# The input projection of a hybrid layer in seven-product form, in three token groups, with the recurrence one group behind

## The chip, the cores and the metric

The kernel runs on one core of a Trainium2 chip. Its time is the device time of one execution in microseconds (us), the median of several runs. The engines are named as in the profile: PE is TensorE's matmul, PEld its weight load, DVE VectorE, ACT ScalarE, POOL GpSimd, SP SyncE, which here only issues DMAs.

## The reference

One layer of a streaming encoder, over 2048 prompt frames (16 tiles of 128 tokens) and 8 streams of 16 frames (one more tile, the "sample" tile, number 16). D_MODEL is 1024.

```
h   = RMSNorm(x);  P = h @ w_in   -> q|k|v (3*512) | z (512) | b, a (4+4) | B, C, H (3*512)
group A: causal conv of 4 taps + SiLU on q, k, v; L2 norm of q and k; beta = sigmoid(b), decay g from a
  per chunk: A = strict lower part of (beta k) k^T * decay;  solve (I + A) [u, w] = [beta v, beta k e^g]
    v_new = u - w S;   o = (q e^g) S + (q k^T * decay) v_new;   S = S e^(g_last) + k_tail^T v_new
  o = RMSNorm_head(o) * SiLU(z)
group B: y = B * causal_conv3(C * H)
x = x + RMSNorm(concat(o, y) @ w_o)
x = x + RMSNorm(SwiGLU(RMSNorm(x)))
```

Outputs are y for prompt and sample tokens, the convolutions' last rows, and the recurrent states (4 heads of 128 x 128) of the prompt and of each stream.

## The kernel before

Every large product is made to f32 accuracy from pieces that run at the fast rate: each operand is split into a high part and a remainder ("hi", "lo"), and a product becomes three matmuls, hi x hi, hi x lo and lo x hi.

**Projection** (0 to 958 us). The 17 tiles are taken in six groups, `GROUPS`: three of three prompt tiles, one of two, and the first, which holds tiles 0, 1 and the sample tile; a group is 384 tokens wide, the one of two 256. For each group the 28 blocks of 128 output channels are made one by one by `project`: 8 parts of the inner dimension times 3 matmuls, 24 in one PSUM bank (`dbank`, three of them), by the helper `mm3` (L141). `weights` casts a block (ACT, L344) and subtracts (L346, half on GpSimd and half on VectorE), and stores the pair in DRAM (`wsplit`), from which most later groups load it. `x_first` and `x_prep` bring a group's x in (L211: the cast of the high part). After each block, `conv_qkv` copies it from PSUM, applies the four taps (`taps`, L372, on VectorE) and a SiLU; the results of a group stay in SBUF.

**Recurrence.** Within each group: `pair_stage` makes k k^T and k q^T of each tile and inverts 32 x 32 blocks on VectorE; `level_stage` (L586, L596, L601) joins the blocks; `chunk_stage` carries the state S from tile to tile: products L641, L648, L655 on the chain from S to the next S with `r` (L643, L644), `yt` (L650) and the update (L658), and L662 and L667 beside it for the output. `sample_stage` does the same for the eight streams. The order is written out by hand: the last chunk of a group is held over and done at the start of the next, so that products of the projection are always at hand between the steps of a chain.

**Output tiles** (958 to 1190). `o_tile` multiplies a tile by `w_o` (L818), adds the residual, and makes the FFN's input; the first eight run alone, the others beside the FFN's preparation. **FFN** (from about 1190): gate-up (L1034, weight sums and splits L1000 to L1010, x parts L938 to L942, combinations L1076 to L1106) in three groups of 6, 6 and 5 tiles, then down (L1192). Both already use the seven-product form.

That form cuts both matrices in two by two blocks (inner dimension in halves, outputs or tokens in halves). Seven products of sums of blocks, instead of eight of blocks, give the four result blocks after some additions. It costs sums of weight blocks, sums of token blocks and combinations of results.

A scheduler orders the instructions of each engine when the program is built. PSUM has eight banks: `psd` 3, `pst` 2, `psg` 2, `pso` 1.

Of the kernel before, what the change touches and what calls it, by code (L numbers as in the profile page):

```python
# [33 lines left out]
WF = W1 + NS * 3  # L34
TLS = True
O_SPLIT = 8
NPD, NPT, NPG = 3, 2, 2
NR, NKV = 3, 2
XKB = 4
# [33 lines left out]
def kernel(  # L73
# [4 lines left out]
    xs0,  # L78
# [29 lines left out]
    mixd = [dram.tile([P, KD, P], F32, name=f"mixd{t}") for t in range(NT)]  # L108
    wsplit = [dram.tile([P, 2, KD, P], F32, name=f"wsplit{j}") for j in range(28)]
# [36 lines left out]
    with ExitStack() as ph:  # L146
# [3 lines left out]
        wk = ph.enter_context(tc.tile_pool(name="wk", bufs=1))  # L150
        small = ph.enter_context(tc.tile_pool(name="small", bufs=2))

        def obank():
            return pso.tile([P, 512], F32, tag="o", name="obank")
# [6 lines left out]

        S = gp.tile([P, H, P], F32, tag="S", name="S_init", bufs=2)
        V.memset(S, 0.0)
        junkq = gp.tile([P, P], BF16, name="junkq")
        junko = gp.tile([P, P], BF16, name="junko")

        inner = ph.enter_context(ExitStack())
        psg = inner.enter_context(tc.tile_pool(name="psg", bufs=NPG, space=PSUM))
        pso = inner.enter_context(tc.tile_pool(name="pso", bufs=8 - NPD - NPT - NPG, space=PSUM))
        dp = inner.enter_context(tc.tile_pool(name="dp", bufs=1))  # L170
        hp = inner.enter_context(tc.tile_pool(name="hp", bufs=KD + 3))
        wp = inner.enter_context(tc.tile_pool(name="wp", bufs=2))
        cp = inner.enter_context(tc.tile_pool(name="cp", bufs=2))

        def spread(r, n):
            c = n * P
            rg = cp.tile([P, W1], F32, tag="xk", name="rg", bufs=XKB)
            V.tensor_mul(rg[:, :c].rearrange("p (t i) -> p t i", t=n), ident.unsqueeze(1).broadcast_to([P, n, P]),
                         r.unsqueeze(2).broadcast_to([P, n, P]))
            ps = tbank()  # L180
            T.matmul(ps[:, :c], ones, rg[:, :c], start=True, stop=True)
            rb = small.tile([P, W1], F32, tag="rb", name="rb")
            A.copy(rb[:, :c], ps[:, :c])
            return rb

        def x_prep(tiles):
            n = len(tiles)
            c = n * P
            ss = small.tile([P, MAXT], F32, tag="xss", name="xss")
            s2 = small.tile([P, MAXT], F32, tag="xs2", name="xs2")  # L190
            for i, t in enumerate(tiles):
                for q in range(2):
                    xt = cp.tile([P, D // 2], F32, tag="x", name="xt")
                    with tc.issue_after(wloads[-20 + 2 * i + q].ins):
                        nc.sync.dma_start(out=xt, in_=x[t, :, q * 512:(q + 1) * 512])
                    if q:
                        V.scalar_tensor_tensor(xt, xt, 1.0, xt, op0=ALU.mult, op1=ALU.mult, accum_out=s2[:, i:i + 1])
                    else:
                        A.activation(xt, xt, AF.Square, accum_out=ss[:, i:i + 1])
            V.tensor_add(ss[:, :n], ss[:, :n], s2[:, :n])  # L200
            r = rstd(small, ss[:, :n], n, 1.0 / D, EPS, "x")
            rb = spread(r, n)
            hi, lo = [], []
            for k in range(KD):
                xk = cp.tile([P, W1], F32, tag="xk", name="xk", bufs=XKB)
                with tc.issue_after(wloads[-11 + k].ins):
                    nc.sync.dma_start(out=xk[:, :c], in_=xT[k, :, tiles[0] * P:tiles[0] * P + c])
                V.tensor_mul(xk[:, :c], xk[:, :c], rb[:, :c])
                h = hp.tile([P, W1], F32R, tag="hi", name="hi")
                l = hp.tile([P, W1], F32R, tag="lo", name="lo")  # L210
                A.activation(h[:, :c], xk[:, :c], AF.Copy, scale=g_pre[:, k:k + 1])  # L211
                V.scalar_tensor_tensor(l[:, :c], xk[:, :c], g_pre[:, k:k + 1],
                                       h[:, :c].bitcast(F32), op0=ALU.mult, op1=ALU.subtract)
                hi.append(h)
                lo.append(l)
            return hi, lo

        def x_first(tiles):
            n = len(tiles)
            c = n * P  # L220
            hi, lo, sqs = [], [], []
            ps = tbank()
            for k in range(KD):
                raw = ubuf[k] if k < len(ubuf) else gp.tile([P, H, P], F32, tag="dt", name="dt", bufs=2 * MAXT)
                raw = raw.rearrange("p h c -> p (h c)")[:, :c]
                nc.sync.dma_start(out=raw, in_=xs0[k])
                l = hp.tile([P, W1], F32R, tag="lo", name="lo")
                h = hp.tile([P, W1], F32R, tag="hi", name="hi")
                A.activation(h[:, :c], raw, AF.Copy, scale=g_pre[:, k:k + 1])
                V.scalar_tensor_tensor(l[:, :c], raw, g_pre[:, k:k + 1],  # L230
                                       h[:, :c].bitcast(F32), op0=ALU.mult, op1=ALU.subtract)
                hi.append(h)
                lo.append(l)
                xk = cp.tile([P, W1], F32, tag="xk", name="xk", bufs=XKB)
                if k % 2:
                    V.tensor_mul(xk[:, :c], raw, raw)
                    V.tensor_add(xk[:, :c], xk[:, :c], sqs[k - 1][:, :c])
                    for i in range(n):
                        T.matmul(ps[:, 2 * i:2 * i + 1], xk[:, i * P:(i + 1) * P], ones[:, 0:1], start=(k == 1 and i == 0),
                                 stop=(k == KD - 1 and i == n - 1), skip_group_check=True)  # L240
                else:
                    A.activation(xk[:, :c], raw, AF.Square)
                sqs.append(xk)
                if k in (0, 3):
                    fetch()
            r = rstd(small, ps[:, :2 * n].rearrange("p (t c) -> p t c", c=2)[:, :, 0], n, 1.0 / D, EPS, "x")
            return hi, lo, spread(r, n)

        def gate_prep(tiles, hi, lo, rb):
            n = len(tiles)  # L250
            npr = sum(t != SAMPLE for t in tiles)
            c = n * P
            ps = bank() if rb is not None else tbank()
            mm3(ps[:16, :c], [(wba[:, k, :], v[k][:, :c]) for k in range(KD) for v in (hi, lo)])
            bsb = cp.tile([P, W1], F32, tag="xk", name="bsb", bufs=XKB)[:16]
            src = ps[:16, :c]
# [297 lines left out]
        def level_stage(tiles, gt):  # L554
            gt["U"] = []
            for i, t in enumerate(tiles):
# [10 lines left out]
                if s:  # L567
                    continue
# [783 lines left out]
```

## Time and profile before

| | |
|---|---|
| runs | 2606.32, 2605.13, 2602.91 us; median 2605.13 |
| span of the profiled execution | 2604.1 us |
| its own time beside the span | not recorded apart: the three runs above are what there is |
| mean granted TensorE clock | 0.984 |
| DMA | 589.41 MB, mean 226 GB/s |
| projection and recurrence | 0 to 958 us |
| first eight output tiles | 958 to 1190 us |
| FFN, with the other output tiles | 1190 to 2604 us |

A row of a group reads: line, engine, operation, output<-inputs, partitions x elements and types, count, then busy time in us, mean ns of one, and the idle time of the engine in front of them with what ended it. For some f32 matmuls two records stand for one product.

### The profile page before, as it was taken

The page shows a single profiled execution, that of the slowest core. Times are in us where ns is not written, and L with a number is a line of the kernel's source. Part 1 is how long each engine was busy: PE and PEld are TensorE (multiplying, and loading weights), DVE is VectorE, ACT ScalarE, POOL GpSimd, SP SyncE. Part 2 cuts the span into 40 slices and gives each one's busy share as a digit, 9 for nine tenths or more (in the row PEclk, how much of TensorE's full clock was granted, in tenths as well). Part 3 has the DMA queues.
Part 4 walks back from the last instruction along what each step waited for, and adds up shares of the span by engine and source line. Part 5 has one row for each costly group of instructions (what it writes and reads, how often), then busy time and mean ns, then how long its engine had stood idle before and what let it go on. Part 6 is the DMA issues. An engine that isn't in the chain of part 4 may idle for free.

```text
span 2604.1 us, 41820 instructions
## 1 busy us (share of the span) xinstructions
PE 2507.8 (96%) x15061; PEld 2337.2 (90%) x15061; DVE 1741.0 (67%) x3502; ACT 1060.3 (41%) x2570; POOL 632.7 (24%) x580
## 2 busy tenths in 40 slices
PE   8989999999999999999999999999999999999998
PEld 7978899999888988788999999999999988787786
DVE  6876666666586655777888864544655554677588
ACT  6546145162656423444434442222433335333343
POOL 3221101010120101214556610000000035455563
PEclk9999999999999989999999999999999999999999
DMA  7966575847666564678877788877988853333465
GB/s 243 308 246 224 200 280 211 271 162 261 200 225 227 192 218 145 219 235 288 301 251 265 264 273 270 273 247 240 301 270 295 271 180 103 119 121 122 129 216 185
DMA packets 320815, 589.41 MB, mean 226 GB/s; under 512 B 55532, under 2 KB 204720, under 8 KB 301792
## 3 DMA queue, kind: packets, MB, share of 16 engines
q1 hardware_dynamic: 182512, 509.28, 57.8%
q10 hardware_dynamic: 138096, 77.46, 9.9%
q8 instruction: 119, 1.95, 0.3%
q14 instruction: 88, 0.72, 0.1%
HBM read 424.60 MB, written 162.05 MB: 225 GB/s over the span
## 4 chain that ended last, share of the span: by engine, by line
PE 67%; DVE 12%; DMA 10%; ACT 5%; issue 3%; POOL 2%; ACTq 1%; SPq 0%; DVEq 0%; POOLq 0%
PE fbank L1034 30%; PE dbank L141 15%; PE fbank L1192 11%; PE tbank L818 2%; PE dbank L818 2%; DMA xt<-in_x 1%; DMA xk<-in_xT 1%; DVE acc L372 1%; POOL dw L891 1%; ACT L407 1%; DVE Ts L548 1%; DVE pr L546 1%; DMA hTd<-ht 1%; DMA partd<-pt 1%; DMA out_y<-xr 1%
## 5 line engine op out<-in xcount | busy, mean ns | idle before, releaser
L1034 PE MATMUL fbank<-xh,fw 128*128 128x384 f32 (+1 forms) x3696 | 902.1, 327 | 9.2 <-ACT m L1068 5.1
L141 PE MATMUL dbank<-hi,w 128*128 128x384 f32 (+1 forms) x2688 | 689.3, 335 | 15.1 <-ACT w L344 6.2
L1034 PEld LDWEIGHTS fbank<-xh,fw 128*128 128x128 f32 x3696 | 653.7, 189 | 11.3 <-ACT m L1068 5.9
L1034 PE MATMUL fbank<-xl,fw 128*128 128x384 f32 (+1 forms) x1848 | 603.7, 327 | 0.0
L141 PEld LDWEIGHTS dbank<-hi,w 128*128 128x128 f32 x2688 | 482.1, 192 | 22.9 <-ACT w L344 6.6
L1192 PE MATMUL fbank<-dw,as 128*128 128x512 f32 x1980 | 460.7, 394 | 7.7 <-ACT dw L889 2.5
L1192 PEld LDWEIGHTS fbank<-dw,as 128*128 128x128 f32 x1980 | 371.6, 188 | 96.5 <-DVE as L1176 3.7
L141 PE MATMUL dbank<-lo,w 128*128 128x384 f32 (+1 forms) x1344 | 446.7, 332 | 0.1
L1034 PEld LDWEIGHTS fbank<-xl,fw 128*128 128x128 f32 x1848 | 348.7, 189 | 0.0
L141 PEld LDWEIGHTS dbank<-lo,w 128*128 128x128 f32 x1344 | 257.1, 191 | 3.3 <-issue 1.2
L1176 POOL TENSOR_TENSOR as<-ar,as 128x256 fp32r<-128x256 f32 (+1 forms) x207 | 186.7, 912 | 281.9 <-ACT as L1173 281.1
L1151 DVE TENSOR_TENSOR acc<-acc,fbank 128x512 f32<-128x512 f32 x248 | 166.3, 682 | 93.6 <-PE fbank L1192 77.9
L891 POOL TENSOR_TENSOR dw<-dr,dw 128x512 fp32r<-128x512 f32 x52 | 77.0, 1493 | 483.7 <-ACT dw L889 483.5
L1173 ACT CAST as<-ar 128x256 fp32r<-128x256 f32 (+1 forms) x288 | 118.1, 427 | 186.2 <-PE fbank L1192 133.8
L1009 ACT CAST fw<-rg 128x512 fp32r<-128x512 f32 x124 | 77.4, 624 | 190.5 <-PE fbank L1034 156.5
L372 DVE SCALAR_TENSOR_TENSOR acc<-R,cw,acc 128x384 f32<-128x384 f32 (+2 forms) x216 | 132.4, 617 | 11.4 <-ACT acc L403 7.7
L346 POOL TENSOR_TENSOR w<-wr,w 128x512 fp32r<-128x512 f32 x49 | 71.7, 1464 | 240.1 <-ACT w L344 189.8
L1081 DVE TENSOR_TENSOR c<-u,fbank 128x384 f32<-128x384 f32 (+1 forms) x66 | 34.9, 528 | 102.1 <-PE fbank L1034 102.1
L1077 DVE TENSOR_TENSOR m<-m,m 128x384 f32<-128x384 f32 (+1 forms) x44 | 23.1, 526 | 98.2 <-ACT m L1070 98.1
L344 ACT CAST w<-wr 128x512 fp32r<-128x512 f32 x98 | 56.5, 615 | 69.9 <-PE dbank L141 27.1
L546 DVE TENSOR_TENSOR pr<-As,Ts 48x31 f32<-48x31 f32 (+25 forms) x186 | 66.3, 356 | 26.4 <-DMA As<-sa 22.1
L1079 ACT ACTIVATE m<-fbank 128x384 f32<-128x384 f32 (+1 forms) x66 | 31.3, 474 | 121.4 <-PE fbank L1034 114.5
(360 smaller groups left out, 3697.2 us busy)
## 6 DMA issues: line engine op xcount, KB each, us to landing
w<-wsplit SPq DMA_DIRECT2D x119, 1024.0 KB, 5.7
fw<-fsplit SPq DMA_DIRECT2D x188, 512.0 KB, 4.6
fsplit<-fw SPq DMA_DIRECT2D x94, 512.0 KB, 4.9
partd<-pt ACTq DMA_DIRECT2D x88, 384.0 KB, 5.9
rg<-in_w_gu SPq DMA_DIRECT2D x62, 512.0 KB, 3.9
wsplit<-w SPq DMA_DIRECT2D x28, 1024.0 KB, 5.5
wr<-in_w_in SPq DMA_DIRECT2D x98, 256.0 KB, 3.4
ar<-partd SPq DMA_DIRECT2D x48, 384.0 KB, 3.5
```

Source lines behind the costliest of these rows:

```text
L141: T.matmul(ps, l, r, start=(i == 0), stop=(i == n - 1))
L346: e.tensor_tensor(out=wl[:, c], in0=wr, in1=wh[:, c].bitcast(F32), op=ALU.subtract)
L372: V.scalar_tensor_tensor(acc, raw(d), w[:, d:d + 1], acc, op0=ALU.mult, op1=ALU.add)
L546: V.tensor_mul(p3, As[:m, j, j + 1:32].unsqueeze(2).broadcast_to([m, a, b]), Ts[:m, j, 0:b].unsqueeze(1).broadcast_to([m, a, b]))
L818: T.matmul(pss[n], m_[:, j, :], w_[k][:, n * 512:(n + 1) * 512], start=(k == 0 and ci == 0), stop=(k == KD - 1 and ci == 2))
L891: e.tensor_tensor(out=w[:, 1], in0=v, in1=w[:, 0].bitcast(F32), op=ALU.subtract)
L1009: A.copy(w[:, 0], v)
L1034: T.matmul(ps, w_[:, c], b_[k][:, :hw], start=(first and k == 0 and ci == 0), stop=(k == KH - 1 and ci == 2), skip_group_check=not first)
L1151: V.tensor_add(dst, dst, ps)
L1173: ins = A.copy(a[:, 0, :n], v)
L1176: e.tensor_tensor(out=a[:, 1, :n], in0=v, in1=a[:, 0, :n].bitcast(F32), op=ALU.subtract)
L1192: T.matmul(ps, a[:, x_, q * P:(q + 1) * P], w[:, y_], start=(start and q == 0 and ci == 0), stop=(q == c - 1 and ci == 2), skip_group_chec ...
```

## The change

The projection takes the FFN's form and its groups. `GROUPS` becomes 0-5, 6-11 and 12-16 (the sample tile is in the last). The 28 blocks become 14 units of two blocks: k0 k1 v0 v1 q0 q1 z0 z1 C0 H0 B0 C1 H1 B1, each with 7 products of 4 inner parts and 3 matmuls, 84 in four `dbank`s (`psd` 4, `pst` 2, `psg` 2). A matmul is 384 wide, or 320 in the last group. Four sums of weight blocks are made for each unit in the first group; four of the seven split pairs are stored and loaded again in the later groups, and three are split anew. The seven parts of x of the next group are made during units 8 to 13, stored in DRAM (`xpd`) and loaded at the group's start. In the first group the products are made on unnormalized x, and each row is scaled afterwards (L487).

k, q, transposed k and v, SiLU(z) and the short convolution's result go to DRAM on SP's queue and are loaded again. The recurrence becomes a generator, `recur`, over the same arithmetic: a pair step per tile, one inversion for a whole group, then a level step and a chunk step per tile. `steps(n)` issues n of its pieces after each unit of the next group; the last group's follow the first eight output tiles, three after each, and the rest after the eighth. The program's `pack` step drops one copy of x and orders `w_in` by units.

```diff
-GROUPS = [[0, 1, 16], [2, 3, 4], [5, 6, 7], [8, 9, 10], [11, 12], [13, 14, 15]]
+GROUPS = [list(range(0, 6)), list(range(6, 12)), list(range(12, 17))]
...
+UNITS = [(kind, half) for kind in "kvqz" for half in range(2)] + [(kind, half) for half in range(2) for kind in "CHB"]
+STEPS = [[0] * 14, [2, 2, 2, 1, 2, 2, 1, 2, 2, 1, 2, 2, 1, 2], [2, 2, 2, 1, 2, 2, 1, 2, 2, 1, 2, 2, 1, 2]]
-NPD, NPT, NPG = 3, 2, 2
+NPD, NPT, NPG = 4, 2, 2
+NR, NACC, NXK, NWR = 4, 2, 8, 7
...
+        def x_load(gi):
+            hw = len(GROUPS[gi]) * P // 2
+            X = {nm: ([], []) for nm in PARTS}
+            for i, nm in enumerate(PARTS):
+                for k in range(KH):
+                    v = xbuf()[:, :hw]
+                    nc.sync.dma_start(out=v, in_=xpd[gi][i, k])
+                    xsplit(X, nm, k, v, hw, G if k % 4 == 3 else V)
+            return X
...
+        def unit_weights(gi, u):
...
+            if gi == 0:
...
+                V.tensor_sub(s[2], a11, a21)
+                V.tensor_add(s[0], a21, a22)
+                V.tensor_sub(s[1], s[0], a11)
+                V.tensor_sub(s[3], a12, s[1])
...
+            for i, (v, e) in enumerate(((a11, G), (s[2], V), (s[0], G), (s[1], V), (a12, G), (a22, G), (s[3], V))):
+                w = wp.tile([P, 2, 512], F32R, tag="w", name="w", bufs=NWR)
+                if v is None:
+                    nc.sync.dma_start(out=w.bitcast(F32), in_=wsplit[u][:, WSL[i]])
+                else:
+                    A.copy(w[:, 0], v)
+                    (V if first else e).tensor_tensor(out=w[:, 1], in0=v, in1=w[:, 0].bitcast(F32), op=ALU.subtract)
+                    if i in WSL:
+                        nc.sync.dma_start(out=wsplit[u][:, WSL[i]], in_=w.bitcast(F32))
+                yield w[:, 0], w[:, 1]
...
+        def unit(gi, u, X, rb, seg):
...
+            b1, b3, b4, b2 = (psd.tile([P, 512], F32, tag="d", name="dbank")[:, :hw] for _ in range(4))
+            for b, w, nm in zip((b1, b3, b4, b2), W, PARTS):
+                product(b, w, X[nm], True)
...
+            A.copy(s1, b1)
+            A.copy(s7, b3)
+            A.copy(s5, b4)
+            product(b1, W[4], X["B21"], False)
+            product(b3, W[5], X["T4"], False)
+            product(b4, W[6], X["B22"], False)
             fetch()
...
+            V.tensor_add(u2, s1, b2)
+            G.tensor_tensor(out=s7, in0=s7, in1=s5, op=ALU.add)
+            for o, f in places(gi, R[0], 0, seg):
+                A.copy(o, f(b1))
+            for o, f in places(gi, R[1], 0, seg):
+                V.tensor_add(o, f(u2), f(b3))
+            for o, f in places(gi, R[1], 1, seg):
+                G.tensor_tensor(out=o, in0=f(s7), in1=f(u2), op=ALU.add)
+            for o, f in places(gi, R[0], 1, seg):
+                V.tensor_add(o, f(u2), f(b4))
+            if rb is not None:
+                for r in R:
+                    G.tensor_tensor(out=r[:, 3:3 + c], in0=r[:, 3:3 + c], in1=rb[:, :c], op=ALU.mult)
+            return R
...
+        def by_tile(dst, src, n):
+            nc.sync.dma_start(out=dst.rearrange("t p c -> p t c"), in_=src[:, :n * P].rearrange("p (t c) -> p t c", c=P))
...
+        def recur(gi, gt):
+            tiles = GROUPS[gi]
+            for i in range(len(tiles)):
+                pair_step(gi, i, gt)
+                yield
+            yield from solve_steps(gi, gt)
+            for i, t in enumerate(tiles):
+                U = level_step(gi, i, gt)
+                yield
+                if t == SAMPLE:
+                    yield from sample_step(gi, i, gt, U)
+                else:
+                    chunk_step(gi, i, gt, U)
+                yield
...
+            for u, (kind, part) in enumerate(UNITS):
+                R = unit(gi, u, X, rb, kind not in "zB")
+                finish_unit(gi, kind, part, R, gt)
+                if (kind, part) == ("k", 1):
+                    gt.update(gate_prep(gi, X, rb))
+                    key_norms(n, gt)
+                if 7 <= u < 13:
+                    next(prep, None)
+                steps(STEPS[gi][u])
...
+            work.append(recur(gi, gt))
...
         for t in range(O_SPLIT):
             o_tile(t)
+            steps(3)
+        steps(99)
+        nc.scalar.dma_start(out=state_p, in_=state_now[0])
```

`product` is a unit's four inner parts by three matmuls (L440). `finish_unit` calls `convolve` (scale on ACT, taps on VectorE over up to 768 tokens, L507) and stores; for H and B it multiplies on GpSimd (L571, L579). `chunk_step`, `level_step`, `pair_step` and `sample_step` are the former stages for one tile, with loads of what was staged at their head; `solve_steps` is the inversion for the 96 blocks of a group.

More of the change, by code (lines that the diff above doesn't have):

```diff
@@ L171 @@
[L171 to L184, printed above, removed]
@@ L203, in x_prep @@
[L203 to L215, printed above, removed]
@@ L216, in x_prep @@
-            return hi, lo
-        def x_first(tiles):
-            n = len(tiles)
[L220 to L247, printed above, removed]
@@ L262, in gate_prep @@
+            ps = tbank()
             for i in range(n):
@@ new lines, with fetch, product @@
+        worder = [(gi, u) for gi in range(len(GROUPS)) for u in range(len(UNITS))]
+        wpend = []
+        def fetch(n=7):
+            if n == 7 and not worder:
+                return
+            if not wpend or len(wpend[-1][2]) == 7:
+                gi, u = worder.pop(0)
+                wpend.append((gi, u, [], unit_weights(gi, u)))
+            for _ in range(n):
+                wpend[-1][2].append(next(wpend[-1][3]))
+        def product(ps, w, b, first):
+            wh, wl = w
+            bh, bl = b
+            hw = ps.shape[-1]
+            for k in range(KH):
+                c = slice(k * P, (k + 1) * P)
+                for ci, (w_, b_) in enumerate(((wh, bh), (wh, bl), (wl, bh))):
+                    T.matmul(ps, w_[:, c], b_[k][:, :hw], start=(first and k == 0 and ci == 0),
+                             stop=(k == KH - 1 and ci == 2), skip_group_check=not first)
```

825 lines of the change are left out of this document (452 added, 373 removed).

## The prediction

> **What bounds the kernel now.** I read the head of the page first, then the chain that ended last, then the table of windows, and only then single instructions.
>
> ```profile
> span 2604.1 us, 41820 instructions
> PE 2507.8 (96%) x15061; PEld 2337.2 (90%) x15061; DVE 1741.0 (67%) x3502; ACT 1060.3 (41%) x2570; POOL 632.7 (24%) x580
> PE 67%; DVE 12%; DMA 10%; ACT 5%; issue 3%; POOL 2%; ACTq 1%; SPq 0%; DVEq 0%; POOLq 0%
> L141 PE MATMUL dbank<-hi,w 128*128 128x384 f32 (+1 forms) x2688 | 689.3, 335 | 15.1 <-ACT w L344 6.2
> ```
>
> TensorE is busy for 96% of the span and carries 67% of the chain; L141 is the projection. So fewer matmuls should pay. But the change touches only what lies before the gate-up product, so its stages must be read alone. In the windows view the columns are: window, its length, busy time (instructions) of PE, PEld, DVE, ACT, POOL, granted clock, DMA share, GB/s. The last row is the same view for L141 alone: PE, clock, DMA share, GB/s.
>
> ```profile
> 0.00:190.00 190.00, 167.27 (x966) 156.64 (x967) 147.98 (x369) 102.12 (x242) 55.72 (x48) 0.95 0.77 266
> 190.00:958.00 768.00, 736.20 (x5425) 703.69 (x5423) 503.33 (x1379) 347.55 (x965) 76.81 (x77) 0.99 0.65 223
> 958.00:1190.00 232.00, 220.94 (x1120) 185.57 (x1121) 152.99 (x303) 93.31 (x233) 36.86 (x47) 0.96 0.60 198
> 1500.00:1600.00 100.00, 100.00 (x579) 100.00 (x578) 58.36 (x105) 36.60 (x77) 6.37 (x5) 1.00 0.84 275
> 2000.00:2100.00 100.00, 100.00 (x683) 100.00 (x683) 52.74 (x102) 30.90 (x66) 0.00 (x0) 1.00 0.84 270
> ...
> 0.00:958.00 958.00, 745.01 (x4128) 0.98 0.68 231
> ```
>
> The projection and the recurrence fill 0 to 958, the first eight output tiles 958 to 1190, and the FFN starts there. TensorE has work throughout; VectorE is at 66% in the second window, GpSimd only at 10%. That spare time of GpSimd is what the change uses up. The two 100-us rows show TensorE without a gap: 100/579 = 172.7 ns for a product 384 wide and 100/683 = 146.4 ns for 320. For 256 wide I divide 4.77 by 40 below and get 119 ns; an x8 there is four 128-column f32 products in two passes, so one head-by-head set of the recurrence is 1.09 us.
>
> ```profile
> 694.04 1.09 PE gbank L641 x8
> 695.13 4.77 PE dbank L141 x40
> ```
>
> **The change part by part.** I forecast when the FFN starts (1190 now) in three terms: first group, second and third group, output tiles. The FFN code itself is unchanged.
>
> *What the products save.* Before: 28 blocks x 24 matmuls x 6 groups = 4032, of which 3360 are 384 wide and 672 are 256: 3360 x 0.1727 + 672 x 0.119 = 660 us. After: 14 units x 84 x 3 = 3528, of which 2352 are 384 wide and 1176 are 320: 406 + 172 = 578 us. At the full rate 82 us go. All of it is on TensorE, so all of it is gain where TensorE remains the bound.
>
> *First group (190 now, for a sixth of the tokens; afterwards six tiles).* TensorE has 1176 x 0.1727 = 203 us of products and some 18 us of gates and transposes, 221 together. But here all weight sums and splits are made afresh, and GpSimd gets much of it. Counted in the changed kernel's order of instructions, GpSimd has 56 operations of 512 elements (weight splits), 54 of 384 (sums of the x parts, splits, combination adds) and 36 of 768 (row scaling at L487, the C·H and B products), 146 in all. VectorE has some 239 operations with two inputs in SBUF: 44 taps 768 wide, 119 of 512, 76 of 384. The trace shows what happens when both meet (timeline and groups; start, duration, engine):
>
> ```profile
> 1312.32 1.74 POOL L1010 TENSOR_TENSOR fw<-rg,fw 128x512 fp32r<-128x512 f32 x1
> 1314.02 1.46 POOL L1082 TENSOR_TENSOR m<-m,u 128x384 f32<-128x384 f32 x1
> 1315.44 1.74 POOL L1010 TENSOR_TENSOR fw<-sA,fw 128x512 fp32r<-128x512 f32 x1
> 1323.88 1.37 POOL L1010 TENSOR_TENSOR fw<-ru,fw 128x512 fp32r<-128x512 f32 x1 [5.13 <-ACT fw L1009]
> 1329.44 1.02 POOL L1077 TENSOR_TENSOR m<-m,m 128x384 f32<-128x384 f32 x1 [4.19 <-issue]
> ...
> 1316.05 1.55 DVE L938 TENSOR_TENSOR ft<-fh 128x384 f32<-128x384 f32 x1
> 1317.63 1.53 DVE L939 TENSOR_TENSOR fh<-fh 128x384 f32<-128x384 f32 x1
> 1319.19 0.56 DVE L942 TENSOR_TENSOR ft<-fh 128x384 f32<-128x384 f32 x1
> 1320.13 0.68 DVE L1001 TENSOR_TENSOR sA<-ru 128x512 f32<-128x512 f32 x1
> ...
> L1083 DVE TENSOR_TENSOR c<-u,fbank 128x384 f32<-128x384 f32 x20 | 10.9, 544 | 0.0
> L372 DVE SCALAR_TENSOR_TENSOR acc<-u,scw,acc 128x384 f32<-128x384 f32 x32 | 19.4, 606 | 0.4
> ...
> 71.36 1.46 DVE L372 SCALAR_TENSOR_TENSOR acc<-R,cw,acc 128x408 f32<-128x408 f32 x1
> ```
>
> Beside GpSimd a 0.56-us VectorE add takes 1.53, almost GpSimd's own duration, and GpSimd's 512-wide operation goes from 1.37 to 1.74; a VectorE add that reads PSUM stays at 0.54. So the two take turns: one VectorE operation slips in per GpSimd operation, at about 0.36 us. GpSimd alone: 56 x 1.37 + 54 x 1.02 + 36 x 2.04 (twice the 384-wide) = 77 + 55 + 73 = 205. The 146 that slip in add 146 x 0.36 = 53. The other 93 VectorE operations cost their own time, by 44 x 1.2 (two 384-wide taps) + 119 x 0.68 + 76 x 0.56 = 176 us over 239 = 0.74 each, 69. With 7 us to the first data (an estimate, a third of the 23 us in which TensorE idles in the first window): 205 + 53 + 69 + 7 = 334, more than TensorE's 221. The lower bound is TensorE at this stage's present pace, 221 x 190/167 = 251; the upper, every operation at its whole length, 205 + 176 + 7 = 388. I take 334, because the unit's adds wait for both engines and only four banks hold unfinished sums.
>
> The Trainium skill, page "SBUF — State Buffer", section "SBUF: two separate sides", says that VectorE with two SBUF inputs and a reading GpSimd operation hold a shared port pair for a whole instruction, and the other blocks fully. The rows above agree that it is exclusive, yet price an admitted operation at 0.36 and not 0.56; by the page's letter this stage would be the 388.
>
> *Second and third group.* Products 203 + 172 = 375 us. Against its ideal the projection now takes 745 us of busy time for 660 + 96 gate matmuls (16) = 676, a factor 1.10: 413. Gates 14. The rest of TensorE's work before 958 is 903.5 - 745.0 = 158.5 us; 9 of it falls into the first group and, below, 66 into the output tiles: 84 remain. Sum 511; idle time as in the second window, 31.8 on 736.2, adds 22. The x parts are in single buffers, so each of the two groups starts with four casts and one subtraction (4 x 0.61 by the row of L211 among the groups, and 1.5 for a subtraction beside GpSimd), about 4 us: 8.
>
> ```profile
> L211 ACT ACTIVATE hi<-xk,vec 128x384 fp32r<-128x384 f32 x32 | 18.5, 613 | 40.8 <-DVE xk L208 28.4 <-DMA mixd<-yo 6.2 <-DVE pr L546 5.3
> w<-wsplit SPq DMA_DIRECT2D x119, 1024.0 KB, 5.7
> ```
>
> Together 541. Staging of keys, queries, values, z and x parts brings, by my count of their sizes, some 76 MB per group, near 280 GB/s; the FFN moves 275 GB/s under a gapless TensorE, so I cost it at nothing, at most 152 MB at the first stage's 266 GB/s = 571, 30 more. The stores stand on SP's queue ahead of weight loads: a store that waits for its SiLU holds the loads behind it. A ring of seven gives a load about six products (12 x 0.1727 x 6 = 12.4 us) against 5.7 us to land; without that cover each late unit loses the difference. Lower end for this term: no extra idle, 519.
>
> *Output tiles (232 now).* Half of the recurrence moves here: in the order of the changed kernel 8 of 16 chunk steps, 5 pair steps and the sample tile stand behind the last projection product. In sets of 1.09 us: 8 x 5 + 5 x 2 + 4 heads x 4 = 66, less the 3 chunk steps that stand here already, 15: 51 x 1.09 = 56, and some 10 for levels and turns: 66. A chunk step's chain is
>
> ```profile
> L643 DVE TENSOR_TENSOR r<-gbank,eG 128x512 f32<-128x512 f32 x13 | 8.8, 680 | 0.1
> L644 DVE TENSOR_TENSOR r<-vt,r 128x512 f32<-128x512 f32 x13 | 8.9, 682 | 0.1
> L650 ACT COPY yt<-gbank 128x512 f32<-128x512 f32 x13 | 7.5, 578 | 5.2 <-PE gbank L648 5.2
> L658 DVE SCALAR_TENSOR_TENSOR S<-S,eL,gbank 128x128 f32<-128x128 f32 x48 | 13.4, 340 | 3.7 <-PE gbank L655 3.7
> ```
>
> three sets, 0.68, 0.68, 0.58 and four times 0.34 = 6.6 us, with 5.5 of TensorE in it if the two side sets fill. Now projection products cover the waits. Afterwards six steps and three sample heads stand with no other matmul between: 1.1 to 3.3 us each, 10 to 30; I take 21, towards the upper end since each step now first loads its operands. 232 + 66 + 21 = 319 (300 to 340).
>
> *Sum.* 334 + 541 + 319 = 1194, against 1190: +4. Two costs I have left at zero, the refill of a unit's banks and the SP queue, can only add; I allow 4. So +8 on the profiled 2604.1, and its time lies 1 below the median of the runs (2605.13): 2613.
>
> **The rivals.** *Faster: the port does not bind.* The place is the first group. If the weight operations spread so that VectorE and GpSimd seldom meet, it ends at TensorE's pace: 251 with today's losses, some 20 more for the start of a six-tile group, 271; the sum falls by 63 to 2550. For it: 1210 to 1500, the FFN's first group, has the same structure with TensorE nearly gapless. Against it: that stretch holds 118 GpSimd operations in 290 us, while here 146 stand on 221. It decides from a first group below about 325.
>
> ```profile
> 1210.00:1500.00 290.00, 283.74 (x1622) 281.96 (x1623) 242.51 (x290) 118.55 (x236) 172.10 (x118) 0.99 0.81 278
> ```
>
> *Slower: four banks.* All four banks of a unit are taken by the next, and VectorE must empty b3 and b4 within two products (4.1 us). A pair of taps 768 wide beside GpSimd stands in front (twice the 1.46 of a 408-wide one, 2.9 us each): if every unit of groups two and three waits 2.9 us, 28 x 2.9 = 81, less the 22 us idle already counted: 2672. *Slower: the whole port.* Every meeting costs its full length, the first group takes 388: 2667. *Slower: the chain behind the last product.* If loads and chains are exposed in all 8 steps and 4 heads at 6.6 us less 3.3, 40 instead of 21, and VectorE, with 270 us of its own work in 319, delays the output tiles' own steps by as much again: 2650. *Nothing saved:* excluded by the count of matmuls, unless the gap rate takes back all 82.
>
> **How the numbers follow.** Forecast case 0.37, port free 0.28, banks 0.16, whole port 0.12, chain 0.07. What can be told from no change is about 0.2%, 5 us. The forecast case reaches from 2580 to 2640; a third of it lies below 2600, a fifth within the 5 us: 0.11 faster, 0.07 same, 0.19 slower. Port free is faster (0.28), the others slower (0.35). Together 0.39, 0.07, 0.54. Port free reaches further down, to 2485 with all three terms at their low ends (251 + 519 + 300 = 1070), so about a tenth of all lies under 2535; banks and whole port together, 2726, put a little less than a tenth above 2690.
>
> **What would show it.** Right: until about 335 TensorE is busy for two thirds, GpSimd over 70% (with L416, L476, L487 near 1.6 and 2.4 us) and VectorE's SBUF-only operations show 1.5 us where 0.6 is their own; groups two and three take 541 with TensorE over 92%; the FFN starts near 1198. Wrong: a first group under 290 with a gapless TensorE; or idle time of L440 released by DVE in every unit of the later groups; or the output tiles over 350; or a changed FFN, which I take as unchanged.

## The result and the profile after

The changed kernel takes 2712.71 us (median of 4 runs, 2707.34 to 2714.14), the kernel before 2605.73 us beside it: 1.0407 times as long, 95% interval 1.0385 to 1.043. The forecast was 2613, its range 2535 to 2690. Slower was the likeliest of the three outcomes (0.54); the size was missed by 100 us. (A slip in the account of the kernel before: four of its six groups hold three prompt tiles, not three. The counts of matmuls go by four.)

The head of the page after, and the second row of its chain:

```profile
span 2711.4 us, 42074 instructions
PE 2478.7 (91%) x14542; PEld 2289.1 (84%) x14542; DVE 1802.4 (66%) x2996; ACT 1125.7 (42%) x2672; POOL 1043.0 (38%) x998
PE 59%; DVE 18%; DMA 11%; issue 5%; ACT 3%; POOL 2%; SPq 1%; ACTq 0%; DVEq 0%; POOLq 0%
PE fbank L1177 30%; PE fbank L1335 11%; PE dbank L440 8%; PE dbank L959 5%; DVE acc L507 3%; DMA dt<-grow 2%; DVE Ts L654 1%; DVE pr L652 1%; DMA wr<-in_w_in 1%; DMA w<-wsplit 1%; DMA qkd<-dt 1%; DVE acc L1294 1%; DVE xr L1354 1%; PE gbank L751 1%; DMA ktd<-kst 1%
```

TensorE is busy 29 us less than before, as fewer matmuls should have it, and the span is 107 us longer: the time went into waiting. The projection's share of the chain fell from 15% to 8%, and VectorE's and the DMAs' rose. The windows view by stage (first group; second and third; from the last projection product to the FFN), in the columns shown before:

```profile
0.00:332.00 332.00, 253.50 (x1307) 239.71 (x1307) 264.84 (x336) 166.46 (x385) 233.81 (x179) 0.88 0.71 236
332.00:900.00 568.00, 517.80 (x3615) 489.39 (x3616) 353.86 (x649) 301.66 (x770) 287.79 (x331) 0.96 0.83 264
900.00:1309.00 409.00, 333.17 (x2080) 276.21 (x2079) 252.43 (x559) 138.59 (x386) 57.30 (x82) 0.87 0.58 190
```

The three terms of the sum were 334, 541 and 319; they are 332, 568 and 409. The FFN starts at 1309.5 instead of 1192.8 and then takes 1402 us instead of 1411, so the loss lies ahead of it: 117 us. The projection ends 56 us earlier than before (900 against 956), and the stage from there to the FFN, the last row, takes 172 us longer (409 against 237). TensorE idles there for 76 us, and its granted clock is 0.87. The longest wait in that stage (columns: who waited for whom, us, times, longest), and its chain:

```profile
PE gbank L681 <- DMA utd<-sT: 28.7, 1, 28.7
...
1070.87 4.05 DMA sa<-AU
1074.97 3.53 DMA As<-sa
...
1098.76 0.35 DVE Ts L654
1099.13 0.33 DVE pr L652
1099.49 0.33 DVE Ts L654
1102.61 2.65 DMA sT<-Ts
1105.28 2.50 DMA utd<-sT
1107.86 0.66 PE gbank L681 x16
```

This is the last group's inversion: a store and a load, 62 VectorE operations (L652, L654) each needing the one ahead, a store and a load. In TensorE's order nothing stands beside it. In the kernel before the inversions lie beside projection products, all six of them (during the last, 901 to 930 us, TensorE is busy without a gap). And it comes late, because the recurrence lags. The first pair product of each group, and the first S product of the last chunk of groups one and two (timeline):

```profile
354.41 0.38 PE L629 MATMUL gbank<-kq 128*128 128x128 f32 x2
...
675.48 0.71 PE L751 MATMUL gbank<-S,kq 128*128 128x128 f32 x4
692.32 0.50 PE L629 MATMUL gbank<-kq 128*128 128x128 f32 x3
...
998.04 1.22 PE L751 MATMUL gbank<-S,kq 128*128 128x128 f32 x4
1007.69 0.72 PE L629 MATMUL gbank<-kq 128*128 128x128 f32 x5
```

A group's recurrence takes 306 to 321 us, longer than the third group's projection (261), so the last group's begins 108 us after the last projection product.

### The profile page after: what moved, and what is told of

It is laid out like the page before. It is cut to its first block, busy times and chain, and to the rows that moved or that the text cites. A ratio compares the mean times of both kernels' runs of the same rounds, so it can differ in the third digit from the quotient of the medians.

```text
span 2711.4 us, 42074 instructions
## 1 busy us (share of the span) xinstructions
PE 2478.7 (91%) x14542; PEld 2289.1 (84%) x14542; DVE 1802.4 (66%) x2996; ACT 1125.7 (42%) x2672; POOL 1043.0 (38%) x998
## 4 chain that ended last, share of the span: by engine, by line
PE 59%; DVE 18%; DMA 11%; issue 5%; ACT 3%; POOL 2%; SPq 1%; ACTq 0%; DVEq 0%; POOLq 0%
PE fbank L1177 30%; PE fbank L1335 11%; PE dbank L440 8%; PE dbank L959 5%; DVE acc L507 3%; DMA dt<-grow 2%; DVE Ts L654 1%; DVE pr L652 1%; DMA wr<-in_w_in 1%; DMA w<-wsplit 1%; DMA qkd<-dt 1%; DVE acc L1294 1%; DVE xr L1354 1%; PE gbank L751 1%; DMA ktd<-kst 1%
## 5 line engine op out<-in xcount | busy, mean ns | idle before, releaser
L440 PE MATMUL dbank<-hi,w 128*128 128x384 f32 (+1 forms) x2352 | 623.4, 344 | 76.6 <-ACT hi L198 26.5
L440 PEld LDWEIGHTS dbank<-hi,w 128*128 128x128 f32 x2352 | 438.0, 198 | 86.7 <-ACT hi L198 30.4
L440 PE MATMUL dbank<-lo,w 128*128 128x384 f32 (+1 forms) x1176 | 402.3, 343 | 8.8 <-DVE lo L199 8.4
L440 PEld LDWEIGHTS dbank<-lo,w 128*128 128x128 f32 x1176 | 233.0, 198 | 15.2 <-DVE lo L199 14.2
L416 POOL TENSOR_TENSOR w<-wr,w 128x512 fp32r<-128x512 f32 x123 | 179.0, 1457 | 112.7 <-ACT w L415 104.1
L507 DVE SCALAR_TENSOR_TENSOR acc<-R,cw,acc 128x768 f32<-128x768 f32 (+1 forms) x108 | 129.2, 1201 | 22.6 <-ACT acc L505 21.9
L959 PE MATMUL dbank<-woh,mh 128*128 128x512 f32 x272 | 97.7, 412 | 10.5 <-DVE xo L969 9.8
L415 ACT CAST w<-wr 128x512 fp32r<-128x512 f32 x126 | 77.8, 619 | 55.9 <-PE dbank L440 22.6
L959 PE MATMUL dbank<-wol,mh 128*128 128x512 f32 x272 | 96.1, 408 | 0.0
L959 PE MATMUL dbank<-woh,ml 128*128 128x512 f32 x272 | 94.7, 403 | 0.0
```

Source lines behind the costliest of these rows:

```text
L415: A.copy(w[:, 0], v)
L416: (V if first else e).tensor_tensor(out=w[:, 1], in0=v, in1=w[:, 0].bitcast(F32), op=ALU.subtract)
L440: T.matmul(ps, w_[:, c], b_[k][:, :hw], start=(first and k == 0 and ci == 0), stop=(k == KH - 1 and ci == 2), skip_group_check=not first)
L507: V.scalar_tensor_tensor(acc[:, :f], R[:, 3 - n + d:3 - n + d + f], w[:, d:d + 1], acc[:, :f], op0=ALU.mult, op1=ALU.add)
L959: T.matmul(pss[n], m_[:, j, :], w_[k][:, n * 512:(n + 1) * 512], start=(k == 0 and ci == 0), stop=(k == KD - 1 and ci == 2))
```

## The experiments

FFN starts and stage lengths below are read from the traces as above; whole times are medians, of two runs each where nothing else is said.

**The recurrence left out, in both kernels (e9, e12).**

```diff
-            work.append(recur(gi, gt))
...
-            nc.sync.dma_start(out=mr[:, :H], in_=mixo[t])
+            nc.sync.dma_start(out=mr[:, :H], in_=mixs[gi][i])
```

This is e9's edit; e12 takes the calls of the pair, level, chunk and sample stages out of the kernel before, and its output tiles, too, read the short convolution's result twice.

> Leaves out the whole recurrence (pair steps, inversions, levels, chunks, sample heads); the output tiles read the short convolution's result twice instead. What is left shows the stages by themselves. Theory K (the recurrence and its waits cost the time, not the units or their four banks): groups two and three fall from 568 to 450-480 (375 us of products x 1.10, gates 14, transposes 16 and the x parts), the output stage from 409 to 225-245, so the FFN starts near 1030. Rival B (four banks, port and x parts hold the units back also without the recurrence): groups two and three stay over 520.

> The kernel before, without its recurrence (pair, level, chunk and sample stages left out; the output tiles read the short convolution's result twice), the counterpart of e9. It prices the projection and the recurrence of the kernel before apart. Theory K (the seven products do save time, and the change loses it in the recurrence): the FFN starts at 1020 to 1060 here against 987 in e9, so the recurrence costs 130 to 170 us in the kernel before and 322 in the changed one. Rival R (the projection saves nothing): it starts at or before 990.

e9 took 2395.05 us, e12 2414.85. The windows of e9 (first the second and third group, then the output tiles) and of e12 (projection, output tiles):

```profile
332.00:763.00 431.00, 419.53 (x2595) 403.03 (x2595) 220.77 (x294) 216.34 (x544) 270.34 (x309) 0.99 0.81 261
763.00:987.00 224.00, 204.84 (x938) 169.78 (x939) 137.49 (x260) 85.99 (x202) 32.60 (x43) 0.95 0.62 206
```
```profile
0.00:791.00 791.00, 742.70 (x4421) 716.39 (x4421) 396.01 (x1001) 371.97 (x931) 87.02 (x71) 0.98 0.75 264
791.00:1002.00 211.00, 202.92 (x938) 167.08 (x937) 137.73 (x260) 86.64 (x202) 33.66 (x41) 0.98 0.63 208
```

This divides the 117 us. Without the recurrence the FFN starts at 987 in the changed kernel and at 1002 in the one before: the seven products bring 15 us. With it, at 1309.5 and 1192.8: the recurrence costs 323 us in the changed kernel and 191 before, 132 more, for the same arithmetic. In e9's groups two and three TensorE is busy for 97% at clock 0.99, so four banks, port and DMA (busy 0.81 of the time) hold back almost nothing there. The recurrence adds 568 - 431 = 137 us to these groups, 98 of it TensorE's busy time and 39 idle, and 409 - 224 = 185 to the output stage.

**One group's recurrence left out (e17: the second's; e16b: the last's).**

```diff
-            work.append(recur(gi, gt))
+            if gi != 1:                      # e16b: gi != 2
+                work.append(recur(gi, gt))
```

The output tiles concerned read the short convolution's result twice; in e16b tile 11's does too, since its last step is issued with the last group. (e16, in which tile 11's was left as it is, has no measured time.)

> Leaves out the recurrence of the second group alone (tiles 6 to 11; their output tiles read the short convolution's result twice). Theory L: the last group's pair steps begin at the last projection product instead of 107 us after it; groups two and three take 490 to 520 instead of 568, the output stage falls by 85 to 115 us, to about 310. Rival (the last group's recurrence alone sets the output stage, whenever it begins): the output stage stays over 370.

> Leaves out the recurrence of the last group alone (tiles 12 to 16; their output tiles and that of tile 11 read the short convolution's result twice). From e17, the last group's recurrence behind the projection costs 343 - 224 = 119 us of output stage and the lagging second group 409 - 343 = 66. Theory L: the two add, so the output stage takes 224 + 66 = 290 us, 275 to 300, and the projection stays at 895 to 905. Rival (the lagging steps alone would find cover beside the output tiles): 225 to 260.

e17 took 2596.60 us (8 runs), e16b 2570.73. From the last projection product to the FFN, e17 and then e16b:

```profile
845.00:1188.00 343.00, 290.20 (x1621) 236.60 (x1620) 217.13 (x466) 118.99 (x311) 50.20 (x69) 0.91 0.61 200
```
```profile
897.00:1163.00 266.00, 246.77 (x1405) 204.91 (x1405) 166.85 (x345) 105.96 (x278) 47.05 (x59) 0.95 0.63 205
```

In e17 the last group's pairs begin at the last projection product (845), and the stage falls by 66; its length of 343 lies 33 above my figure and 27 under the rival's. In e16b it is 266: the last group's recurrence alone costs 343 - 224 = 119, the second group's lagging steps alone 266 - 224 = 42. They do not add as I had put it: together 161, and the other 24 of the 185 arise only where both are there and the one delays the other.

**The inversion and the cover (e1, e2).**

```diff
-            for j in range(31):
+            for j in range(31 if gi < 2 else 0):      # e1
```
```diff
+O_FIRST = 12                                          # e2
...
-        for t in range(O_SPLIT):
+        for t in range(O_FIRST):
             o_tile(t)
-            steps(3)
+            steps(2)
...
-                o_tile(t)
+                if t >= O_FIRST:
+                    o_tile(t)
```

> Leaves out the 31 steps of the block inversion of the last group alone (its T stays the identity, so the last group's recurrence is computed with other numbers; every other instruction stays). Theory A (the time was lost because this inversion is a serial chain on VectorE that now stands behind the last projection product with no matmul beside it): the 28.7 us gap in front of L681 shrinks to the two DMA hops, under 8 us, and the whole falls by 20 to 28 us, to about 2688. Rival B (VectorE and the short steps of the chain are the bound of the output stage wherever the inversion stands, so the gap only moves): the whole falls by under 8 us.

> Nothing is left out: twelve output tiles instead of eight stand between the pieces of the last group's recurrence, with two pieces after each instead of three; the FFN's preparation then runs beside tiles 12 to 16 alone. Theory A (uncovered chains): four more tiles of 48 matmuls, 4 x 10.9 = 44 us, cover the inversion and part of the chunk steps; TensorE's idle time from 900 to the start of the FFN falls by 30 to 45 us, the whole to 2670 to 2685. Rival B (the output stage is bound by VectorE's work): the idle time stays, the whole changes by under 8 us. Rival C (FFN preparation loses its cover): 10 to 20 us slower.

e1 took 2696.54 us, 16 less: between the theories. Its gap shrank, but not to the DMA hops (waits of TensorE, e1):

```profile
PE gbank L681 <- DMA AU<-aud: 17.1, 1, 17.1
```

Without the inversion the level step's load of AU is next late. e2 took 2707.24, 5 less: a miss. Its trace shows why: the pair steps of the last group still begin at 1000, and when its inversion starts (1088) eleven of the twelve output tiles have gone as cover for the second group's lag and for the pair steps; the twelfth begins at 1090, and the gap behind it is still 18.4 us.

**The written pace (e5, e6).**

```diff
-STEPS = [[0] * 14, [2, 2, 2, 1, 2, 2, 1, 2, 2, 1, 2, 2, 1, 2], [2, 2, 2, 1, 2, 2, 1, 2, 2, 1, 2, 2, 1, 2]]
+STEPS = [[0] * 14, [3] * 14, [3] * 14]                         # e5
+STEPS = [[0] * 14, [3] * 14, [4] * 6 + [2] * 7 + [1]]          # e6, recur of the last group begun after its q units
```

> Nothing is left out: three pieces of the recurrence after every unit of groups two and three instead of one or two, so by the written order a group's 22 pieces end in the middle of the next group. Theory K (a group's recurrence is one serial sequence whose pieces wait for their own single-buffered loads and for VectorE, some 300 us per group, whatever the written pace): the last projection product still finds several chunk steps of the second group open, the last group's pair steps begin 60 us or more after it, the whole moves by under 25 us. Rival W (the written pace of 24 pieces per 14 units sets it): all chunk steps of the second group stand inside the projection, the last group's pair steps begin within 15 us of its end, the whole falls by 60 to 100 us.

> Nothing is left out: as e5, with four pieces per unit in the last group's first six units, and the last group's own recurrence begins after its q units, so its pair steps and inversion lie beside its z, B, C and H units. Theory A+K (the loss of the output stage is the last group's pair steps, inversion and chain, which start 107 us after the projection's end and find no cover): the 28.7 us gap goes, the stage from the last projection product to the FFN falls from 409 to 310-345; the projection gets 10 to 25 us longer by the work moved into it; the whole falls by 45 to 80 us, to 2635-2665. Rival V (VectorE is the bound of projection and output stage together): the projection gets longer by what the output stage gets shorter, the whole moves by under 15 us.

Both missed: 2743.49 and 2762.87 us, 31 and 50 slower. The output stage got shorter (387 and 379 instead of 409), but groups two and three longer (608 and 649 instead of 568), and in both the second group's first pair product comes at 657 to 661, 31 to 35 earlier, while its last chunk comes 30 earlier in e6 (968) and 11 later in e5 (1009). TensorE keeps the order in which the program was built, so a piece that stands earlier holds the projection products behind it: in both, group three's first product comes 83 us after group two's last one, instead of 23, with the first group's last chunk steps and the second group's first pair steps between them (waits of TensorE, e5):

```profile
PE gbank L629 <- DVE AU L632: 21.8, 3, 20.0
```

For e5 that is theory K in kind (the last group's pairs begin 89 us after the projection's end), though the whole moved by more than its 25 us; for e6 it is neither theory, since the last group's pairs still began only at 982, right at the projection's end.

**Buffers, banks, queues (e10, e13, e14, e15).** e10 gives dt, AU and utd two buffers (`bufs=2`), e13 sets `NPD, NPT, NPG = 4, 1, 3`, e14 issues the recurrence's loads with `nc.scalar` instead of `nc.sync`, e15 is e10, e13 and e2 together (with three pieces again after each output tile from the seventh).

> Nothing is left out: the staged tiles dt, AU and utd get two buffers instead of one, paid for with one x buffer and by letting the turn's two tiles share the tags r and kl. Theory K1 (a piece of the recurrence waits above all for its own load into a single buffer): pair steps come every 10 to 13 us instead of 18, a group's recurrence takes 250 to 270 us instead of 305 to 320, the whole falls by 25 to 60 us. Rival K2 (the pieces wait for VectorE's queue, SP's queue and the order of TensorE): under 10 us.

> Nothing is left out: the recurrence's PSUM banks go from two to three, the transposes' from two to one. Theory K3 (level and chunk steps stand one behind the other because two banks carry both, each product between 3 to 4 us of projection products, some 28 us per tile): a tile's level and chunk take 22 to 25 us in group two's units, the lag of 107 us behind the last projection product falls under 85, the whole falls by 10 to 40 us. Rival T (the one bank for transposes holds the units): groups two and three longer than 575, the whole slower by 5 to 30.

> Nothing is left out: the recurrence's loads are issued by ACT instead of SP. Theory Q (the pieces wait because their loads stand in SP's queue behind stores and weight loads that wait): pair steps every 12 to 14 us instead of 18, the whole falls by 20 to 50 us. Rival (the loads are there in time, or ACT now waits with its casts behind them): within 8 us, or slower by 10 to 40.

> Nothing is left out: two buffers (e10), the third bank (e13) and twelve output tiles between the last pieces (e2) together. By theory K the lag shortens and more of the tail is covered: 2640 to 2680. If e13 loses by its single transpose bank: 2690 to 2720. Neither beats the kernel before.

e10 took 2693.22 us, 19 less, between the theories: pair steps of the first group come every 14 us instead of 18, but the group's recurrence still lasts 320, as its inversion (438 to 498) and its tiles (28 us each) do not follow. The gain is in the output stage, 385 us instead of 409, where the last group's first level product comes at 1090 instead of 1108. e13 took 2762.71: the single transpose bank lengthens the first group to 359 us; a tile's level and chunk in group two take 25 us against 29 (from one first level product to the next), so theory K3 is at most half tested. e14 took 2739.89, slower by 27, with pair steps as before. e15 took 2747.40 and follows e13. What makes a tile take 26 to 28 us beside projection products (from one chunk's first S product to the next, the changed kernel and e10) and 14 behind them stays open.

**The x parts (e4, e7).** e4 issues the first eight loads of a group's x parts before unit 12 of the group ahead; e7 also makes the x parts in units 2 to 7.

```diff
-                if 7 <= u < 13:
+                if 2 <= u < 8:                         # e7
                     next(prep, None)
```

> Nothing is left out: the first eight of the 28 x-part loads of a group are issued before unit 12 of the group ahead, so they stand in SP's queue in front of its last stores. Theory S (the gaps of 13.1 and 23.4 us at the two group boundaries come from x loads that stand behind a store waiting for its data): both shrink to under 8 us, the whole falls by 20 to 28 us. Rival (the boundary is set by the casts and subtractions of the x parts, whose single buffers come free late): the gaps stay over 10 us, the whole falls by under 8.

> Nothing is left out: the next group's x parts are made in units 2 to 7 instead of 7 to 12, and the first eight of their loads are issued before unit 10, so x_prep's stores no longer stand in SP's queue at the end of the group. Theory S2 (the loads at a boundary wait because the stores of the same x parts are issued until 635 us, 4 us before the boundary): the boundary gaps of 13 and 23 us shrink to under 10, groups two and three together take 540 to 550 instead of 568, the whole falls by 15 to 30 us. Rival (the moved VectorE and GpSimd work delays the first group's units by as much): groups two and three shorter, the first longer, the whole within 8 us.

e4 took 2713.54, no change: the stores of the same x parts were still being issued at 633, so the loads could not be earlier. e7 took 2712.32, and is the most telling of the misses. Its first group ends at 321 instead of 332 and its second takes 281 instead of 307, so the boundary does go; but the third takes 298 instead of 261, and the last projection product comes at 900 as before. The pair steps of groups two and three start at 697 and 1001, much as in the changed kernel (692 and 1008), and four chunk steps of the first group stand behind the boundary instead of two: of the 37 us by which the third group grew, TensorE is busy for 25 and idle for 12. What the projection gained it gave back to the recurrence. The FFN started 10 us earlier (1299) but took 1412 us instead of 1402, so the whole stayed the same. (e8, e6 and e7 together, took 2751.60, another miss.)

**The first group (e3, e11).**

```diff
-            if rb is not None:
+            if rb is not None and False:               # e3
```
```diff
                 for r in R:
-                    G.tensor_tensor(out=r[:, 3:3 + c], in0=r[:, 3:3 + c], in1=rb[:, :c], op=ALU.mult)
+                    for _ in range(3):                 # e11
+                        G.memset(r[:, 3:3 + c], 0.0)
```

> Leaves out the 28 row scalings of GpSimd in the first group (L487), so the first group's results are unnormalized. Theory P (the first group is set by the turns of GpSimd and VectorE at one port): 28 x (2.04 + 0.36) = 67 us of turns go; the first group ends at 265 to 285 instead of 332, the whole falls by 45 to 65 us. Rival Q (the first group is set by the arrival of x, the weight loads and the four banks): it ends above 315, the whole falls by under 20 us.

> Leaves out the row scaling of the first group and puts three GpSimd memsets of the same 768 elements in its place (the first group's values become zero): much the same time on GpSimd and the same waits, but nothing is read from SBUF. If it is the turns at the port that e3 took away, the first group ends at 295 to 312, near e3's 300; if it is GpSimd's own time, at 325 to 335 as in the changed kernel.

e3 took 2669.58, 43 less, and its first group ends at 300; e11 took 2666.81 and ends it at 303. The first group of the changed kernel, then of e11 up to 302 us (groups by form):

```profile
L487 POOL TENSOR_TENSOR R<-R,rb 128x768 f32<-128x768 f32 x27 | 50.9, 1892 | 4.3 <-DVE R L484 3.3 <-ACT R L478 1.0
L507 DVE SCALAR_TENSOR_TENSOR acc<-R,cw,acc 128x768 f32<-128x768 f32 x36 | 50.8, 1420 | 0.6 <-ACT acc L505 0.3
L416 DVE TENSOR_TENSOR w<-sD,w 128x512 fp32r<-128x512 f32 x14 | 18.1, 1296 | 2.7 <-ACT w L415 2.6
```
```profile
L488 POOL MEMSET R<- 128x768 f32 x77 | 55.6, 740 | 8.4 <-DVE R L484 6.1 <-DVE R L480 1.6
L508 DVE SCALAR_TENSOR_TENSOR acc<-R,cw,acc 128x768 f32<-128x768 f32 x36 | 44.2, 1236 | 0.4 <-ACT acc L506 0.2
L416 DVE TENSOR_TENSOR w<-sD,w 128x512 fp32r<-128x512 f32 x14 | 11.8, 843 | 1.9 <-ACT w L415 1.9
```

GpSimd spends as long on memsets as on the scaling (it is busy 231 us in e11's first group, 234 in the changed kernel's), and the stage still gets 29 us shorter. VectorE's operations get shorter with it: the splits of sD fall from 1296 to 843 ns, those of sB and sC less (956 to 925 and 989 to 919); all three together take 45.3 us in the changed kernel, 37.7 in e11 and 36.3 in e3. So it is the reading, not GpSimd's time: that the two engines hold each other up where both read is shown. The Trainium skill, page "SBUF — State Buffer", section "Who interferes with whom", says so: a VectorE instruction with two SBUF inputs contends with a GpSimd instruction that reads SBUF, not with one that only writes it. The trace agrees. But of the 67 us that I priced for these 28 operations only 32 went, so e3 fell between the theories.

## Why the prediction was wrong, step by step

*The products.* 82 us at the full rate was right as a count. 15 arrive, by e9 and e12. In the projection 28 do (763 us against 791): in e9's first group TensorE is idle for 81 of the 332 us. In the output stage 13 are lost again (224 against 211, the recurrence left out of both), by what was not tested.

*First group, 334: it took 332, in part by luck.* The mechanism named is at work (e11), but the sum is less good than it looks: 28 scalings were priced at 67 us and were worth 32, though one took 1.89 us, within 0.15 of the 2.04 in the sum. Against that the sum held 7 us to the first data, where TensorE waits 9.7 us for the first weights and 10.3 for x in its first 24, with the scaling or without it (9.6 and 9.2 in e3). What else of the 332 belongs to which engine no run divides. Of the signs that the prediction named, GpSimd is busy for 70% as forecast, TensorE for 76% and not two thirds, and L487 takes 1.89 us and not 2.4. The rival of the whole port (388) and that of the free port (271) both fell. By the letter of the Trainium skill's page "SBUF — State Buffer", section "SBUF: two separate sides", a whole block, the sum would have been 388; the trace stands 56 below.

*Second and third group, 541: they took 568.* The units were priced well, even high: without the recurrence they take 431, where 541 less the 84 gives 457. The step that fell short here is "84 us of other work on TensorE": I let the recurrence cost there only what TensorE computes in it. It costs 137, of which 39 are idle time. The rival of the four banks is excluded by e9, and in the changed kernel itself TensorE waits only 9 us in these groups for VectorE's additions out of the banks (L480, L484), where the rival had 81.

*Output tiles, 319: they took 409. This is the step that failed.* I counted the moved matmuls, 66 us, and for the chain 21 us as "six steps and three sample heads with no other matmul between". What stands behind the last projection product was counted rightly: four chunk steps of the second group are there (914 to 998 us), and five pair steps. But the 90 us over the forecast are 44 of idle time (76, where 11 before and the 21 make 32) and 46 of busy time (TensorE is busy 112 us longer than before, not 66). Three things were missing. First, the inversion: no term holds it as a link of the chain, though its row (L546, 186 operations) was on the page of the kernel before; it is 24 us, and with its DMAs the 28.7-us gap, and without it (e1) the whole is 16 us shorter. Second, that the last group cannot begin at the projection's end: I never added up a group's pieces. In the first group they are 92 us from the first pair step to the last, 84 from there to the first level product, with the inversion between, and 145 for the six tiles, 321 us together (306 in the second group), against the 261 us of the third group's projection, beside which the second group's had to fit. Without the second group's recurrence (e17) the stage is 66 us shorter, and the last group's alone then still costs 119. Third, TensorE's own time: its granted clock is 0.87 in this stage against 0.96 before, and the products of the output tiles keep it busy for 205 us here and for 194 in e9 (clock 0.95), so some 10 of the 46 go with the lower clock; the rest lies in the recurrence's products, and no run divides it. The rival "the chain behind the last product" named the right place at 2650 and a chance of 0.07; measured, the stage is 90 longer than forecast and not 38. That the output tiles take over 350 us was among the prediction's own signs of being wrong.

*The FFN,* forecast as unchanged, became 9 us shorter (1402 against 1411). With the same FFN code it takes 1401.9 to 1414.8 us in the runs above (but 1429 and 1433 in e13 and e15), so these 9 us cannot be put down to the change.

*The range* reached up by adding two rivals of groups two and three. It held no case in which the output stage took more than 357, since no term had the recurrence as a sequence of its own.

## What to carry to other kernels

When a serial sequence is moved to run beside other work, add up its own length first, piece by piece with its loads and stores, and compare it with the work it is to hide behind; if it is longer, it can become the clock of that stretch, and what is made faster beside it (here e7) gains nothing. Here pair steps that stood 2 to 10 us apart within a group now stand 12 to 18 us apart on average, staged through DRAM in single buffers (a second buffer, e10, brings 18 to 14), and the same arithmetic cost 323 us instead of 191; how much of that is the staging and how much the order, no run divides. What stands at the end of such a sequence, here the last group, must be priced as if it stood alone.

## What the runs showed of the hardware that was not expected

A GpSimd memset of 768 elements (0.74 us) leaves VectorE's two-input operations almost alone, where a GpSimd multiplication of the same tile does not: the splits of sD take 0.76 us with neither (e3), 0.84 with memsets (e11) and 1.30 with the multiplication, the taps (L507, L508 in e11) 1.20, 1.24 and 1.42. And for the stage these multiplications cost less than their own time: 28 of 1.89 us, 53 us together, were worth 32.
